# One layer in blocks of 768, 704 and 640 tokens with 47 ring tiles, column sums by transposition, shared tiles for the last norm and the plain gate in place

## The chip, the core and the metric

The kernel is one program on one core of a Trainium2 chip. The metric is the device time of one execution in microseconds (us). A core has five engines with instruction queues of their own: TensorE (PE, matmuls; the profile lists its weight loads as PEld), VectorE (DVE), ScalarE (ACT), GpSimd (POOL) and SyncE (SP). SP and POOL also issue nearly all DMA transfers here: SP the weights, POOL everything with a token dimension (spills to and reloads from DRAM, inputs, outputs).

## What is computed

One layer runs over 2048 prompt tokens and, with its own state, over 64 sample tokens. All data is float32, D_MODEL = 1024.

```python
h = rms_norm(x, g_pre)
vA, bA, cA, zA, q, f, iv, zB, gA, gB = split_cols(h @ w_in)        # ten pieces of 1024 columns
u = cA * vA;  conv = causal_conv3([conv_hist, u], conv_w)
yA = (silu(zA) * bA * conv) @ w_a_out
fg = lb + (1 - lb) * sigmoid(f);  logf = log(fg);  kk = 1 - fg;  qq = silu(q) * 128**-0.5
# 8 heads of 128 x 128, chunks of 64 tokens, state S carried from chunk to chunk:
#   att = tril(qe ke^T);  o = att v + (q exp b) S;  S = exp(b_last) S + (k exp(b_last - b))^T v
o = o * rsqrt(mean(o * o) + EPS) * g_onorm
yB = (o * silu(zB)) @ w_b_out
out = (sigmoid(gA) * yA + sigmoid(gB) * yB) @ w_o
x = x + rms_norm(out, g_post)
x = x + (p @ w_ple_proj) * sigmoid(rms_norm(x, g_ple) @ w_ple_gate)
```

The outputs are x for both sequences, the last two rows of u and the last S of each.

## The kernel before, in words

**Layout.** Everything is kept feature-major: a tile has 128 features (partitions) by the tokens of a block. The tokens stand in one row of 2112: prompt tokens up to CUT, then the 64 sample tokens, then the rest of the prompt. `plan()` (L46) cuts this row into NB = 3 blocks of BN = 704 tokens, each of two halves of HN = 352. A block's tokens fall into chunks of 64, and its `groups` are pairs of chunks (128 tokens) and, where a run has an odd number of chunks, one single. With CUT = 1344 each block has five pairs and one single. `parts` are up to four pairs, or one single: three parts a block (4 pairs, 1 pair, 1 single).

**Ring.** Nearly all working tiles come from one pool, `ring` (RING = 52 tiles of 708 columns, taken with `rt()`), and smaller half-wide ones from `hf()` (9). A new tile takes over the place of one that is no longer read; its first writer, a DMA among them, waits for that one's last reader. PSUM has five banks for gemms (`ps_gemm`) and three for the rest (`ps_attn`).

**Gemms.** Each float32 product is made of three fp32r matmuls: both operands are split into a rounded `hi` and a remainder `lo` (`split`, L188), and hi\*hi + hi\*lo + lo\*hi are summed. A group of two column blocks by one 1024-deep operand is computed in seven half-size products in place of eight (`sgroup`, L349, matmuls L363 to L365; `in_turn`, matmuls L496 to L498, takes whole stages product by product). `gemm` and its relatives use eight (`mm3`, L529 to L531), `plain_group` too (L433 to L435). Weights come as `raw` tiles by SP, ACT casts them to `hi` (L218), and their `lo` comes from DRAM where an earlier block has written it; block 0 makes the `lo` parts and the weight sums and writes them out. `prepare_sums` makes the sums of w_a_out and w_b_out (during block 0), w_o and w_ple_gate (beside `path_a` of blocks 1 and 2): POOL loads four tiles per group, DVE combines them (L337 to L343), POOL writes them out.

**Stages of a block.** (1) `gates`: sigmoid(gA) and sigmoid(gB), spilled; a number of these groups, LEAD = 7, runs at the end of the block before, the others fill in between the heads. (2) `path_b`: for each of 8 heads two sgroups (`head_prep`), and `head_attn` in four steps for every part: transposes of kb and vt and the scores (L925 to L952), state updates (L958 to L979), outputs and their norm (L994 to L1003), transposition back (L1008). The steps are `hooks`: one is called after each of the products of later sgroups, so attention matmuls stand between gemm matmuls, in PE's order. (3) `path_a`: 8 times two sgroups, with the convolution. (4) W_A, W_B, W_O: in block 0 plain gemms (`merge`, `final_out`), in block 1 W_A and W_B `in_turn` and W_O plain, in block 2 all `in_turn`. During W_O the next block's operands are made (`operands`: x loads at L643, scaling at L693, splits), the last two column blocks of W_O going k by k, so that the operand tiles of `mg` come free one k after the other. (5) `final_norm`: two norms with `rms` (`col_rstd`, `spread`); each step is a hook of the next block's gates. (6) the gate gemm W_G: for block 0 plain in `final_gate` after LEAD gates; for block 1 plain, at the end of block 2; for block 2 `in_turn` (`gate_in_turn`). Ahead of block 0 stands a prologue with the PLE gemms of blocks 0 and 1 (L1058 to L1060).

**Norms.** `col_rstd` (L614) sums the 128 partitions of a tile by matmuls with a column of ones as the moving operand, one per 128 tokens (L620), so that the sums come out as columns of PSUM, from which DVE and POOL make 1/sqrt. `spread` (L599) transposes the columns back over all partitions. `final_norm` of the last block runs once for each half, each with its own acc2, rs, rs2 and its own x tiles.

**Order.** `behind_all`, `placed` and `paced` put instructions behind named others in an engine's order. Each engine runs its queue in that order.

## Time and profile before

| | |
|---|---|
| median of three timed runs | 2609.88 us (2609.3 to 2610.56) |
| profiled execution | 2611.61 us, its span 2609.9 us |
| mean granted TensorE clock | 1.000 |
| DMA over the span | 745.99 MB, mean 286 GB/s |

How to read the rows shown below. A window row has: the stretch in us, its length, then for PE, PEld, DVE, ACT and POOL the busy time and, in brackets, how many instructions ran, then the granted clock, the mean busy share of the 16 DMA engines (which can pass 1 where packets overlap) and GB/s. A group row has: line, engine, operation, output<-inputs, shapes, xcount, then busy us and mean ns of one, then the idle time before them and what ended it. A row of waits reads: engine, what waited, what it waited for, us in total, how often, the longest. A timeline row has start, duration, instruction and, in brackets, the idle time before it and what ended it. Matmuls overlap in the pipeline, so their durations are longer than their spacing. A float32 matmul that isn't fp32r shows as two records, a transposition and an fp32r matmul as one.

### The profile page before, as it was taken

How to read it: one execution, taken by the hardware profiler on the slowest of the kernel's cores; microseconds unless marked ns; L12 is line 12 of the kernel's file. 1: busy time of each engine (PE TensorE's matmuls, PEld its weight loads, DVE VectorE, ACT ScalarE, POOL GpSimd, SP SyncE). 2: the span in 40 equal slices, each digit the busy share in tenths (PEclk: the TensorE clock that was granted, in tenths of full speed). 3: DMA queues.
4: the chain of work that ended last, by engine and by line, in shares of the span. 5: the costliest groups of instructions: out<-in, count | busy, mean ns of one | idle time of the engine just before them, and what ended most of it. 6: DMA issues, size and time to landing. Idle time of an engine off the chain costs nothing.

```text
span 2609.9 us, 47443 instructions
## 1 busy us (share of the span) xinstructions
PE 2588.6 (99%) x16562; PEld 2572.5 (99%) x16562; DVE 1667.1 (64%) x3232; ACT 1538.9 (59%) x2940; POOL 392.6 (15%) x722
## 2 busy tenths in 40 slices
PE   8999999999999999999999999999999999999999
PEld 8999999999999999999999999999999999999998
DVE  8778888888766555455545568553455544568756
ACT  6666665554434644677745556466667744555746
POOL 2000000200441212101112211021000101210220
PEclk9999999999999999999999999999999999999999
DMA  7687787898988997777789989599776789999977
GB/s 285 234 275 259 251 285 257 306 318 286 342 292 285 351 320 259 248 231 224 226 288 359 381 311 312 193 359 358 229 230 220 224 256 335 377 321 309 339 256 240
DMA packets 362672, 745.99 MB, mean 286 GB/s; under 512 B 44640, under 2 KB 49280, under 8 KB 362432
## 3 DMA queue, kind: packets, MB, share of 16 engines
q1 hardware_dynamic: 319680, 579.55, 65.4%
q0 software_dynamic: 42464, 163.37, 17.0%
q8 instruction: 130, 2.13, 0.3%
q14 instruction: 110, 0.90, 0.1%
q10 hardware_dynamic: 288, 0.05, 0.0%
HBM read 531.74 MB, written 211.04 MB: 285 GB/s over the span
## 4 chain that ended last, share of the span: by engine, by line
PE 89%; DMA 3%; DVE 2%; issue 2%; ACT 1%; POOL 1%; DVEq 0%; POOLq 0%; ACTq 0%; SPq 0%
PE pg L363 19%; PE pg L365 19%; PE pg L364 19%; PE pg L496 4%; PE pg L497 4%; PE pg L498 4%; PE pg L530 4%; PE pg L531 4%; PE pg L529 4%; PE pa L994 1%; PE pa L958 1%; PE pa L996 1%; PE pa L944 1%; DMA r<-w_blk 1%; DMA raw<-S 1%
## 5 line engine op out<-in xcount | busy, mean ns | idle before, releaser
L363 PE MATMUL pg<-r,hi 128*128 128x352 f32 x3304 | 1092.9, 331 | 4.6 <-DVE r L409 3.1
L364 PE MATMUL pg<-r,hi 128*128 128x352 f32 x3304 | 1067.6, 323 | 0.0
L365 PE MATMUL pg<-r,lo 128*128 128x352 f32 x2356 | 762.1, 323 | 1.2 <-DMA lo<-low 1.2
L218 ACT CAST hi<-raw 128x512 fp32r<-128x512 f32 x720 | 445.0, 620 | 499.8 <-PE pg L364 165.6
L363 PEld LDWEIGHTS pg<-r,hi 128*128 128x128 f32 x3304 | 622.2, 188 | 9.1 <-DVE r L409 3.2
L364 PEld LDWEIGHTS pg<-r,hi 128*128 128x128 f32 x3304 | 622.2, 188 | 0.0
L365 PEld LDWEIGHTS pg<-r,lo 128*128 128x128 f32 x2356 | 442.3, 188 | 1.8 <-DMA lo<-low 1.7
L365 PE MATMUL pg<-r,s 128*128 128x352 f32 x948 | 306.2, 323 | 0.1
L530 PE MATMUL pg<-r,hi 128*128 128x352 f32 x768 | 248.4, 324 | 0.0
L529 PE MATMUL pg<-r,hi 128*128 128x352 f32 x768 | 248.1, 323 | 0.0
L188 ACT CAST hi<-raw 128x512 fp32r<-128x512 f32 x218 | 134.6, 621 | 153.1 <-PE pg L364 53.5
L188 DVE TENSOR_TENSOR r<-r,r 128x352 fp32r<-128x352 f32 (+3 forms) x298 | 182.8, 637 | 62.7 <-ACT r L188 61.7
L497 PE MATMUL pg<-r,hi 128*128 128x352 f32 x672 | 217.3, 325 | 0.0
L496 PE MATMUL pg<-r,hi 128*128 128x352 f32 x672 | 213.6, 325 | 0.1
L531 PE MATMUL pg<-r,lo 128*128 128x352 f32 x656 | 211.9, 323 | 0.1
L188 ACT CAST r<-r 128x352 fp32r<-128x352 f32 (+3 forms) x298 | 162.2, 580 | 56.9 <-DVE r L1114 15.4
L188 DVE TENSOR_TENSOR lo<-raw,hi 128x512 fp32r<-128x512 f32 x218 | 149.4, 687 | 63.5 <-ACT hi L188 55.2
L365 PEld LDWEIGHTS pg<-r,s 128*128 128x128 f32 x948 | 178.4, 188 | 0.4 <-DMA s<-low 0.4
L188 ACT CAST hi<-s 128x512 fp32r<-128x512 f32 x160 | 98.5, 621 | 123.0 <-PE pg L364 105.8
L377 ACT COPY hf<-pg 128x352 f32<-128x352 f32 x354 | 157.1, 446 | 11.5 <-PE pg L365 10.9
L530 PEld LDWEIGHTS pg<-r,hi 128*128 128x128 f32 x768 | 144.3, 188 | 0.3 <-DVE r L188 0.2
L529 PEld LDWEIGHTS pg<-r,hi 128*128 128x128 f32 x768 | 144.2, 188 | 0.0
(367 smaller groups left out, 4157.0 us busy)
## 6 DMA issues: line engine op xcount, KB each, us to landing
raw<-w_blk SPq DMA_DIRECT2D x570, 256.0 KB, 4.2
lo<-low SPq DMA_DIRECT2D x411, 256.0 KB, 4.4
raw<-S SPq DMA_DIRECT2D x408, 256.0 KB, 4.4
low<-lo SPq DMA_DIRECT2D x314, 256.0 KB, 3.7
s<-low SPq DMA_DIRECT2D x309, 256.0 KB, 4.2
S<-s SPq DMA_DIRECT2D x152, 256.0 KB, 3.2
r<-w_blk POOLq DMA_DIRECT2D x64, 256.0 KB, 7.3
S<-r POOLq DMA_DIRECT2D x64, 256.0 KB, 5.8
```

The costliest lines, as they stand in the source:

```text
L188: return A.copy(hi, src).ins, V.tensor_tensor(lo, src, hi.bitcast(F32), ALU.subtract).ins
L218: A.copy(hi, raw)
L363: add(hi[:, k, :], xhi, start=start and k == 0, stop=False)
L364: add(hi[:, k, :], xlo, start=False, stop=False)
L365: last[0] = add(lo[:, k, :], xhi, start=False, stop=k == KH - 1).ins
L377: copied = A.copy(got[n], ps[bank])
L496: add(hi[:, k, :], xhi, start=start and k == 0, stop=False)
L497: add(hi[:, k, :], xlo, start=False, stop=False)
L498: last[0] = add(lo[:, k, :], xhi, start=False, stop=k == KH - 1).ins
L529: T.matmul(ps, hi[:, k % 4, :], xhi[:, c], start=k == ks[0], stop=False)
L530: T.matmul(ps, hi[:, k % 4, :], xlo[:, c], start=False, stop=False)
L531: last[0] = T.matmul(ps, lo[:, k % 4, :], xhi[:, c], start=False, stop=k == ks[-1]).ins
```

## The change

Blocks get sizes of their own, 768, 704 and 640 tokens, with CUT = 1408; all widths follow from the block at hand (`wide`, set by `width_of` and `of_block`), tiles are as wide as the widest block (772 columns), and there are 47 of them. The groups become 6 pairs; 5 pairs and the sample's single; 5 pairs, in parts of 4 + 2, 4 + 1 + single, 4 + 1. Four places follow suit: `head_prep` handles any even number of pairs in its swapped layout, `head_attn` copies v that way for parts of two, the scores of a single pair go to the first slot of `att`, and the first head of block 0 has two empty hooks instead of one after its third step.

Besides, `col_rstd` transposes tiles and lets DVE reduce them; the two halves of the last block's norm share acc2, rs, rs2 and full-width x tiles, which the first half loads; `final_gate` multiplies and adds in the tile of `p`, half by half with an `hf` tile for the sigmoid, and asks for x when the gemm begins instead of one gemm ahead.

```diff
-CUT = 1344
-BN = 704
-HN = BN // 2
-NB = TOK // BN
-RING = 52
+SIZES = (768, 704, 640)
+CUT = SIZES[0] + SIZES[1] - DEC
+BMAX = max(SIZES)
+HMAX = BMAX // 2
+RING = 47
...
-    def rt(n=BN, dt=F32):
-        t = ring.tile([P, BN + 4], dt, tag="r", name=nm("r"))
-        return t if n is None else t[:, :n]
+    def rt(n=None, dt=F32):
+        return ring.tile([P, BMAX + 4], dt, tag="r", name=nm("r"))[:, : n or wide[0]]
...
         with placed():
             for i, o in tiles_of(n):
-                T.matmul(pc[:, i : i + 1], acc[:, o : o + P], ones, start=True, stop=True)
-        rstd_of(pc[:, : cols.shape[1]], cols, 1.0 / D)
+                T.transpose(pc[:, i * P : i * P + P], acc[:, o : o + P], ident)
+        nt = cols.shape[1]
+        V.tensor_reduce(cols, cols3(pc, nt), axis=mybir.AxisListType.X, op=ALU.add)
+        rstd_of(cols, cols, 1.0 / D)
...
-            V.tensor_tensor(kb[:, 4 * P :], sf[:, 4 * P :], lg[:, 4 * P :], ALU.mult)
...
+            if n > nsw * P:
+                V.tensor_tensor(kb[:, nsw * P :], sf[:, nsw * P :], lg[:, nsw * P :], ALU.mult)
...
+            if npair > nsw:
+                rest = kb[:, nsw * P : np1].rearrange("p (g c t) -> p g c t", c=2, t=CH)[:, :, 0, :]
+                V.tensor_tensor(rest, ka3[:, nsw:npair, :], f2[:, nsw:npair].unsqueeze(2).to_broadcast([P, 1, CH]), ALU.mult)
+                if nch == 2 * npair:
+                    V.memset(ka[:, nch // 2 * CH : nch // 2 * CH + CH], 0.0)
...
                 if step == 2:
-                    hooks.append(None)
+                    hooks.extend([None] * (2 if first and hd == 0 else 1))
...
-        acc2, rs, rs2 = rt(), rt(), rt()
-        xks = []
-
-        def fetch():
-            j = len(xks)
-            if j < KB:
-                xks.append(rt())
-                G.dma_start(xks[j][:, c], x_fm[j * P : (j + 1) * P, segs[0]["t0"] : segs[0]["t0"] + n])
-
-        for _ in range(3 if bl["last"] else 4):
-            fetch()
+        (acc2, rs, rs2), xks = common["tiles"], common["xks"]
+        ahead = 3 if bl["last"] else 4
+
+        def fetch(upto):
+            while len(xks) < min(upto, KB):
+                xks.append(load_x(bl, len(xks)))
+
+        fetch(ahead)
...
-        def fetch(j):
-            return [reload(kept[kind, j]) for kind in "xp"] if j < KB else None
-
-        nxt = fetch(0)
+        nxt = reload(kept["p", 0])
         for j in range(KB):
+            pj, xj = nxt, reload(kept["x", j])
             pss = gemm(W_G + j, h2, segs)
-            (xj, pj), nxt = nxt, fetch(j + 1)
-            t = rt()
+            nxt = reload(kept["p", j + 1]) if j + 1 < KB else None
             for s, ps in zip(segs, pss):
-                A.activation(t[:, cols_of(s)], ps, AF.Sigmoid)
-            V.tensor_tensor(t, pj, t, ALU.mult)
-            V.tensor_tensor(t, t, xj, ALU.add)
-            queue.dma_start(y_fm[j * P : (j + 1) * P, bl["t0"] : bl["t0"] + BN], t)
+                gate = hf()
+                A.activation(gate, ps, AF.Sigmoid)
+                V.tensor_tensor(pj[:, cols_of(s)], pj[:, cols_of(s)], gate, ALU.mult)
+            V.tensor_tensor(pj, pj, xj, ALU.add)
+            queue.dma_start(y_fm[j * P : (j + 1) * P, bl["t0"] : bl["t0"] + bl["n"]], pj)
...
                 if (idx, n) == (W_O, 4):
-                    norms = [final_norm(bl, [s], xo, acc, h2, None, True) for s in segs]
+                    common = {}
+                    norms = [of_block(bl, final_norm(bl, [s], xo, acc, h2, None, True, common)) for s in segs]
```

## The prediction

> **What bounds the kernel now.** I read the page's busy times and its chain of waits first, then PE's own waits, then a window in which PE never stops.

> ```profile
> span 2609.9 us, 47443 instructions
> PE 2588.6 (99%) x16562; PEld 2572.5 (99%) x16562; DVE 1667.1 (64%) x3232; ACT 1538.9 (59%) x2940; POOL 392.6 (15%) x722
> PE 89%; DMA 3%; DVE 2%; issue 2%; ACT 1%; POOL 1%; DVEq 0%; POOLq 0%; ACTq 0%; SPq 0%
> ...
> PE pa L1058 <- ACT r L188: 6.6, 1, 6.6
> PE pg L363 <- DVE r L409: 3.1, 9, 0.6
> PE pa L1008 <- DVE r L1003: 1.7, 1, 1.7
> PE pg L363 <- ACT hi L218: 1.5, 2, 0.7
> ...
> 550.00:600.00 50.00, 50.00 (x312) 50.00 (x311) 43.92 (x73) 24.42 (x45) 1.27 (x4) 1.00 0.86 291
> ```

> TensorE is the bound: 89% of the chain, 99% busy, and its four longest waits make only 12.9 us. So the time is a sum over matmul records, each at its spacing from start to start (the durations in the groups overlap). The window gives 50.00 / 312 = 160.3 ns for a gemm matmul of 352 columns. The change is worth the change of that sum, plus whatever PE then waits for. The profiled execution took 2611.6 us (span 2609.9); the timed runs have their median at 2609.9, 1.7 below it, and I carry the difference over to the median. A measurement here can tell about 0.2%, 5.2 us, from no change.

> **Columns: +3.1 us.** The blocks stay three, so the number of gemm matmuls stays and only their widths move. Counted in the loops, in triples like L363 to L365: block 0 has 1064 by seven products, 64 in plain_group, 512 in plain gemms (W_A, W_B, W_O, W_G) and 32 for PLE, 1672; block 1 has 1120 + 224 + 256 + 32 = 1632; block 2, by seven products throughout, 1120 + 448 + 32 = 1600. The group agrees with its share: 1064 + 1120 + 1120 = 3304.

> ```profile
> L364 PE MATMUL pg<-r,hi 128*128 128x352 f32 x3304 | 1067.6, 323 | 0.0
> ```

> Widths go from 352 everywhere to 384, 352, 320: 3 x 32 x (1672 - 1600) = 6912 columns more, because the widest block is the one that skips the seven-product scheme most. At 160.3 / 352 = 0.455 ns a column, +3.1. Were a part of the spacing fixed, at most the 0.11 us that 128-column records take (next rows), the slope would be (160.3 - 110) / (352 - 128) = 0.22 ns and the price +1.6. I take 3.1, since this shape's own row gives it.

> **Attention groups: -9.7 us.** Today each block has five pairs of chunks and one single; after, the blocks have 6 pairs, 5 pairs and a single, 5 pairs. Per head two singles go and one pair comes. Either costs 11 PE records: three transposes of one record (L925, L927, L1008) and four matmuls of two (L944, L958, L994, L996); the number of L943 matmuls stays.

> ```profile
> 304.13 0.32 PE L365 MATMUL pg<-r,lo 128*128 128x352 f32 x1
> 304.30 0.61 PE L994 MATMUL pa<-r,att 128*128 128x128 f32 x4
> 304.74 0.39 PE L996 MATMUL pa<-r,r 128*128 128x128 f32 x2
> 304.96 0.39 PE L994 MATMUL pa<-r,att 128*128 128x128 f32 x2
> 305.19 0.39 PE L996 MATMUL pa<-r,r 128*128 128x128 f32 x2
> ...
> L994 PE MATMUL pa<-lone,att 128*128 128x128 f32 x48 | 9.2, 273 | 0.0
> ```

> Four records take 304.74 - 304.30 = 0.44 us, two 0.22: 0.11 a record. 8 heads x 11 x 0.11 = 9.7. DVE and ACT lose the singles' work too, which hides behind PE anyway. With two parts rather than three, p_o and the transpose of its norm (L1008) stand three hooks apart instead of four. In between run Square, reduce, pow and multiply:

> ```profile
> L1000 ACT ACTIVATE r<-pa 128x512 f32<-128x512 f32 x24 | 14.4, 600 | 14.7 <-PE pa L996 14.7
> L1001 DVE TENSOR_REDUCE ms<-r 128x4 f32<-128x512 f32 x24 | 16.5, 686 | 30.5 <-ACT r L1000 30.5
> L593 POOL TENSOR_TENSOR ms<-ms,mhalf 128x4 f32<-128x4 f32 (+2 forms) x72 | 53.1, 738 | 295.3 <-DVE ms L591 293.6
> L1003 DVE TENSOR_TENSOR r<-pa,ms 128x512 f32<-128x512 f32 x24 | 16.6, 692 | 27.2 <-POOL ms L593 27.2
> ```

> That is 2.7 us; three hooks are 36 matmuls, 5.2 us even at 320 columns. Covered; without the cover it would be a stall at each of 8 heads. Block 0's first head gets one empty hook more: it is the head where PE waits 1.7 us for L1003 today. I book -1.7 (0 if the chain is late again).

> **Column sums: -4.6, and +0.5 in the prologue.** A matmul against `ones` runs as two records, a transpose as one: 84 become 42, 42 x 0.11 = 4.6.

> ```profile
> L620 PE MATMUL pa<-ones,r 128*128 128x1 f32 x84 | 10.1, 244 | 0.1
> L1001 DVE TENSOR_REDUCE ms<-lone 64x1 f32<-64x128 f32 x24 | 6.8, 283 | 0.8
> ```

> The 14 new reduces over 3x128 lie between 283 and 686 ns, about 0.55 us each, and wait in DVE's order. Twelve stand behind hooks with gemm work around them. Two stand in the prologue, where the first matmul waits 6.6 us anyway: exposed they cost 1.1, hidden 0; with the 9% wider first loads and splits I take +0.5 (0 to 2).

> [...]

> **Head starts of block 0: -1.** PE waits 3.1 us in nine places for DVE's sink (L409). With 9% more time per product and no single to serve, DVE gains room; 0 to -3.1, I take -1.

> **Gate in place, shared norm tiles: 0.** The plain gate splits one DVE multiply into halves, beside 24 matmuls per half gemm. Its x is asked for only when its own gemm starts, and a gemm (48 matmuls at 175 ns) takes 8.4 us:

> ```profile
> r<-x POOLq DMA_DIRECT2D x16, 352.0 KB, 5.4
> ```

> 5.4 us lie behind that. If a tile comes late, DVE is late, and next ACT's `hf` tiles, nine of them; PE is reached last. The last norm's second half loads no x of its own, 8 issues less on POOL's queue.

> **DMA in block 2: +5.6.** Block 2's matmuls get 9% faster, but each still needs the same weight bytes. Two stretches have the DMA engines full already:

> ```profile
> 1700.00:1800.00 100.00, 99.89 (x629) 99.10 (x628) 47.48 (x76) 59.71 (x110) 21.82 (x38) 1.00 1.02 381
> 2200.00:2300.00 100.00, 98.98 (x613) 98.46 (x612) 54.49 (x94) 50.97 (x99) 21.44 (x44) 1.00 1.02 378
> ...
> 1740.00:1750.00 10.00, 10.00 (x64) 10.00 (x63) 4.42 (x9) 6.03 (x13) 1.62 (x3) 1.00 1.04 405
> 1780.00:1790.00 10.00, 10.00 (x64) 10.00 (x63) 2.71 (x5) 4.84 (x10) 1.22 (x3) 1.00 1.04 406
> ...
> DVE r L337 <- DMA r<-w_blk: 51.3, 10, 8.7
> ```

> The first is block 1's norm (x loads, two spills a tile) beside block 2's first gates. Its 38.1 MB, of which only the gates' spills shrink (0.5 MB), would have to pass in 90.9 us, 414 GB/s. At some 400, just below the fullest rows, they take 94.0: +3.1 of lost gain. The second is prepare_sums beside path_a: 37.8 MB at 400 take 94.5, +3.6; part may slip, as W_G needs the sums much later, but DVE stands up to 8.7 us before L337 and its sinks queue behind it, so I take +2.5. Ends: 0 each (all of it slips), 9.1 each (no gain at all).

> **Ring of 47: +2.** Near the end of W_O, counted in the code, live tiles are 16 of mg, 7 for each finished pair of the next block's operands, 11 for the pair in work, xo and the sums. The last pair's x loads wait for PE to release mg:

> ```profile
> 830.54 1.07 POOL L643 DMA_DIRECT2D r<-x_fm  x2 [28.38 <-PE pg L531]
> 1677.62 1.07 POOL L643 DMA_DIRECT2D r<-x_fm  x2 [28.36 <-PE pg L531]
> 840.75 0.94 DVE L693 SCALAR_TENSOR_TENSOR r<-r,vec,r 128x704 f32<-128x704 f32 x1
> 844.95 0.51 ACT L188 CAST r<-r 128x352 fp32r<-128x352 f32 x1
> ...
> 851.26 0.43 PE L363 MATMUL pg<-r,hi 128*128 128x352 f32 x1 [0.74 <-ACT hi L218]
> ```

> Each k of the by-k gemm releases two tiles in 12 matmuls, 1.9 us (2.1 in block 0). Five tiles fewer put the loads 2.5 steps, about 5 us, later, and POOL's norm loads behind them. x is scaled at 841.7 and ACT casts it only at 844.95, behind other work: 3.2 us of cover. So some 1.8 us a block end, twice, less 1.4 for block 0's longer steps: +2. Ends: 0, and 10 with the cover gone.

> **Sum:** 3.1 - 9.7 - 1.7 - 4.6 + 0.5 - 1 + 5.6 + 2 = -5.8. 2611.6 - 5.8 = 2605.8 for the profiled execution, 2604.1 for the median: **2604**.

> **Rivals.** *The DMA engines hold block 2 back* (slower). If they pass no more than the 381 and 378 GB/s of both stretches, PE keeps its old pace there: 2 x 9.1 instead of 5.6, +12.6, **2617**. It decides once the ceiling lies below some 385. For it: a share of 1.02 over whole stretches; against: 405 for ten microseconds. [...] *The ring exposes the block ends*: +10 for +2, **2612**; for it the waits of 28 us, against it the 3.2 us of cover. *Nothing comes in the way*: 5.6 and 2 fall to 0, **2596**; for it that PE stood 0.1 us in all between 1700 and 1800. *Block 2's matmuls don't get shorter*, so that the change doesn't do what it says: 4800 x 14.6 ns more, **2674**; the 0.11 of narrower records speaks against a floor at 160. *Losses that only offset the gain*, several of these in part: **2609**.

> **Chances.** Forecast 0.38, nothing in the way 0.14, ring 0.18, DMA 0.17, offset 0.11, no shorter matmuls 0.02. The forecast's own spread, 2599 to 2608, leaves three quarters of it beyond 5.2 us: faster 0.14 + 0.28 = 0.42; slower 0.17 + 0.02 + half the ring's 0.09 = 0.28; same the rest, 0.30. Range 2595 to 2618: it takes in all but the far end of each unknown cost.

> **What would show it.** Spacing of 175, 160 and 146 ns in plain stretches of the three blocks; 88 records fewer in attention (L994's `lone` form x16 for x48), 42 transposes for L620; no wait before L1008. DMA: gaps of PE in block 2's first gates and in path_a, ended by DMA or L409, over 5.6 us in all mean the rival. Ring: L643's last loads later than one k into W_O's last gemm, and a PE gap in each next block's first product over 1 us. The prediction is wrong if those gaps exceed the 14 us that the shorter record list saves, or if the spacing at 320 stays near 160.

## The result and the profile after

The change makes the kernel slower by about 0.2%: 2615.88 us median of 17 runs (2612.61 to 2618.3) against 2610.55 of 17 runs of the kernel before (2607.92 to 2613.15), a ratio of 1.002 with the interval 1.0012 to 1.0027. The profiled execution took 2618.3 us, its span is 2616.6.

From the page of the changed kernel, its span, the busy times and the engines' shares of the chain that ended last; below them the longest of TensorE's own waits (engine, tile and line, what it waited for, us in total, times, the longest):

```profile
span 2616.6 us, 47076 instructions
PE 2584.3 (99%) x16432; PEld 2564.4 (98%) x16432; DVE 1648.8 (63%) x3165; ACT 1525.9 (58%) x2908; POOL 376.6 (14%) x698
PE 82%; DMA 5%; ACT 4%; DVE 3%; issue 2%; POOL 1%; ACTq 0%; POOLq 0%; SPq 0%; DVEq 0%
```

```profile
PE pa L1084 <- ACT r L207: 6.9, 1, 6.9
PE pg L384 <- DMA lo<-low: 4.1, 3, 2.2
PE pg L382 <- DVE r L429: 3.8, 4, 1.8
PE pa L953 <- DVE r L429: 2.0, 7, 0.3
PE pa L624 <- POOL cols L613: 1.8, 6, 0.5
PE pg L549 <- ACT r L207: 1.6, 2, 1.2
```

TensorE runs 130 matmul records fewer and is busy 4 us less, yet the span is 6.7 us longer. Its share of the chain fell from 89% to 82%; DMA, ScalarE and VectorE took the difference. The waits ahead of L384, L953, L624 and L549 are new or longer; the one ahead of block 0's first norm transposes (L1008 before, L1034 now) is gone.

Windows of the changed kernel without a gap, one in each block, then the two stretches of block 2 that the prediction called full (us; length; busy time and instructions of PE, PEld, DVE, ACT, POOL; granted clock; DMA share; GB/s):

```profile
500.00:550.00 50.00, 50.00 (x287) 50.00 (x287) 41.20 (x74) 26.67 (x57) 5.21 (x10) 1.00 0.86 298
1380.00:1430.00 50.00, 50.00 (x317) 49.93 (x316) 21.93 (x48) 25.45 (x54) 9.78 (x20) 1.00 0.86 294
1830.00:1880.00 50.00, 50.00 (x343) 50.00 (x342) 18.38 (x32) 30.20 (x56) 7.57 (x14) 1.00 1.04 391
...
1770.00:1860.00 90.00, 86.85 (x583) 85.59 (x582) 46.66 (x77) 54.68 (x104) 21.26 (x37) 0.98 1.01 384
2230.00:2330.00 100.00, 95.55 (x636) 94.38 (x635) 56.37 (x101) 51.21 (x102) 21.44 (x45) 0.98 1.04 389
```

The matmuls did get their forecast pace, 50 / 287 = 174 ns, 158 and 146 ns (the second has a few records of attention in it; the median spacing there is 161). In the two stretches where the DMA engines are full (share 1.01 and 1.04, 384 and 389 GB/s), TensorE now stands for 3.1 and 4.5 us.

**A wait that the sum did not have.** In block 2, each head's transposes of vt (L953) wait for VectorE. The timeline of the changed kernel at one head (start, us, engine and line, idle before in brackets):

```profile
2022.91 0.82 DVE L908 TENSOR_TENSOR r<-r,qc 128x640 f32<-128x640 f32 x1
...
2023.27 0.60 PE L951 MATMUL pa<-ident,r 128*128 128x128 f32 x4
...
2024.06 0.48 DVE L429 TENSOR_TENSOR r<-hf,hf 128x320 f32<-128x320 f32 x1
2024.19 0.84 PE L953 MATMUL pa<-ident,r 128*128 128x128 f32 x4 [0.33 <-DVE r L429]
...
2026.13 0.40 PE L382 MATMUL pg<-r,hi 128*128 128x320 f32 x1
```

VectorE is still at the end of `scaled` (L908) when TensorE is done with the head's last product, so the two adds that make vt (L429) come late: the second ends 1.27 us after L951's start. In the kernel before, the same add (L409 there) ended 0.86 us ahead of the transposes of kb:

```profile
2008.00 0.52 DVE L409 TENSOR_TENSOR r<-hf,hf 128x352 f32<-128x352 f32 x1
...
2009.38 0.60 PE L925 MATMUL pa<-ident,r 128*128 128x128 f32 x4
2009.81 0.60 PE L927 MATMUL pa<-ident,r 128*128 128x128 f32 x4
```

From L951 to the next product (L382) the burst takes 2026.13 - 2023.27 = 2.86 us; an undisturbed one 2.14 (below, one_slot). Seven of block 2's eight heads pay this, 4.9 us in all; the sum of the 24 bursts of this kind, eight in each block, rose from 51.1 to 56.0 us.

**A stall that costs more than itself.** Windows of 2 us around the longest gap in block 2's path_a (1.83 us idle ahead of 2294.62, ended by L429):

```profile
2290.00:2292.00 2.00, 2.00 (x14) 1.80 (x13) 0.76 (x2) 0.18 (x1) 0.00 (x0) 1.00 1.05 384
2292.00:2294.00 2.00, 0.79 (x6) 0.52 (x4) 1.93 (x4) 0.62 (x1) 1.44 (x3) 1.00 1.06 388
2294.00:2296.00 2.00, 1.38 (x8) 1.41 (x9) 1.85 (x5) 0.00 (x0) 0.72 (x2) 0.85 1.04 391
2296.00:2298.00 2.00, 2.00 (x9) 2.00 (x9) 1.08 (x2) 1.98 (x4) 0.18 (x1) 0.50 1.05 416
2298.00:2300.00 2.00, 2.00 (x13) 2.00 (x12) 1.23 (x3) 1.52 (x5) 0.00 (x0) 0.79 1.04 410
```

After the gap the granted clock is 0.50 for 3.4 us: nothing is waited for, PE is busy throughout, and 9 matmuls fit into 2 us where 14 did (267 ns each). The changed kernel's trace has three such spells after its start (1701, 1803 and 2295 us), each right behind a gap of over 2 us (2.47 and 2.15 from start to start) or behind several close together; the trace of before has none between its start and its last matmul. Each costs about 1.5 us: some 12 matmuls stand at half clock throughout and take 120 ns more each, 1.44, and the two at its ends add about 0.1.

### The profile page after: what moved, and what is told of

Same layout as the page of the kernel before. It is cut to its first block, busy times and chain, and to the rows that moved or that the text cites. A ratio compares the mean times of both kernels' runs of the same rounds, so it can differ in the third digit from the quotient of the medians.

```text
span 2616.6 us, 47076 instructions
## 1 busy us (share of the span) xinstructions
PE 2584.3 (99%) x16432; PEld 2564.4 (98%) x16432; DVE 1648.8 (63%) x3165; ACT 1525.9 (58%) x2908; POOL 376.6 (14%) x698
## 4 chain that ended last, share of the span: by engine, by line
PE 82%; DMA 5%; ACT 4%; DVE 3%; issue 2%; POOL 1%; ACTq 0%; POOLq 0%; SPq 0%; DVEq 0%
PE pg L382 16%; PE pg L383 16%; PE pg L384 16%; PE pg L551 5%; PE pg L550 5%; PE pg L549 5%; PE pg L516 4%; PE pg L517 4%; PE pg L518 3%; DMA raw<-S 2%; DMA r<-w_blk 1%; PE pa L984 1%; PE pa L1020 1%; PE pa L970 1%; ACT hi L237 1%
## 5 line engine op out<-in xcount | busy, mean ns | idle before, releaser
L382 PE MATMUL pg<-r,hi 128*128 128x320 f32 (+2 forms) x3304 | 1087.5, 329 | 5.5 <-DVE r L429 3.8
L383 PE MATMUL pg<-r,hi 128*128 128x320 f32 (+2 forms) x3304 | 1069.3, 324 | 0.0
L384 PE MATMUL pg<-r,lo 128*128 128x384 f32 (+2 forms) x2356 | 766.9, 326 | 4.1 <-DMA lo<-low 4.1
L382 PEld LDWEIGHTS pg<-r,hi 128*128 128x128 f32 x3304 | 622.6, 188 | 7.9 <-issue 4.7
L383 PEld LDWEIGHTS pg<-r,hi 128*128 128x128 f32 x3304 | 622.7, 188 | 0.2 <-DVE r L207 0.2
L384 PEld LDWEIGHTS pg<-r,lo 128*128 128x128 f32 x2356 | 443.2, 188 | 5.1 <-DMA lo<-low 5.1
L384 PE MATMUL pg<-r,s 128*128 128x352 f32 (+1 forms) x948 | 299.3, 316 | 1.0 <-DMA s<-low 1.0
L549 PE MATMUL pg<-r,hi 128*128 128x384 f32 (+1 forms) x768 | 256.1, 334 | 1.6 <-ACT r L207 1.6
L550 PE MATMUL pg<-r,hi 128*128 128x384 f32 (+1 forms) x768 | 256.1, 334 | 0.1
L207 ACT CAST hi<-raw 128x512 fp32r<-128x512 f32 x218 | 134.7, 620 | 178.2 <-PE pg L550 57.9
L207 DVE TENSOR_TENSOR r<-r,r 128x320 fp32r<-128x320 f32 (+7 forms) x298 | 182.0, 633 | 64.9 <-ACT r L207 63.9
L551 PE MATMUL pg<-r,lo 128*128 128x384 f32 (+1 forms) x656 | 219.9, 335 | 0.0
L517 PE MATMUL pg<-r,hi 128*128 128x320 f32 (+1 forms) x672 | 211.1, 316 | 0.2 <-DVE r L207 0.2
L516 PE MATMUL pg<-r,hi 128*128 128x320 f32 (+1 forms) x672 | 206.0, 316 | 0.9 <-ACT r L207 0.8
L207 DVE TENSOR_TENSOR lo<-raw,hi 128x512 fp32r<-128x512 f32 x218 | 149.3, 686 | 63.1 <-ACT hi L207 60.4
L207 ACT CAST r<-r 128x320 fp32r<-128x320 f32 (+7 forms) x298 | 161.0, 576 | 46.0 <-DVE r L715 12.7
L207 ACT CAST hi<-s 128x512 fp32r<-128x512 f32 x160 | 98.0, 618 | 145.7 <-PE pg L383 130.8
L384 PEld LDWEIGHTS pg<-r,s 128*128 128x128 f32 x948 | 178.5, 188 | 1.8 <-DMA s<-low 1.8
L396 ACT COPY hf<-pg 128x352 f32<-128x352 f32 (+2 forms) x354 | 156.7, 444 | 3.8 <-PE pg L384 3.6
L207 DVE TENSOR_TENSOR lo<-s,hi 128x512 fp32r<-128x512 f32 x160 | 110.1, 689 | 68.9 <-ACT hi L207 67.3
L549 PEld LDWEIGHTS pg<-r,hi 128*128 128x128 f32 x768 | 144.8, 189 | 2.2 <-ACT r L207 2.2
```

Of the source, the lines that this page charges most:

```text
L207: return A.copy(hi, src).ins, V.tensor_tensor(lo, src, hi.bitcast(F32), ALU.subtract).ins
L382: add(hi[:, k, :], xhi, start=start and k == 0, stop=False)
L383: add(hi[:, k, :], xlo, start=False, stop=False)
L384: last[0] = add(lo[:, k, :], xhi, start=False, stop=k == KH - 1).ins
L396: copied = A.copy(got[n], ps[bank])
L516: add(hi[:, k, :], xhi, start=start and k == 0, stop=False)
```

## The experiments

Two theories of the loss were put to the test, with rivals. *Covers*: work of nearly fixed length on ScalarE, VectorE and the DMA engines lay hidden behind TensorE's products; products that are 9% shorter, in a block of two attention parts, no longer hide it. Against it: the ring of 47, the column sums by transposition, or DMA alone. Ratios are to the kernel before.

| run | blocks, and what differs from the change | median us | ratio, interval |
|---|---|---|---|
| after_again | none | 2615.97 | 1.0019, 1.001 to 1.0028 |
| old_sizes_52 | 3 x 704, ring 52 | 2612.29 | 0.9998, 0.999 to 1.0007 |
| old_sizes_47 | 3 x 704 | 2611.8 | 1.0001, 0.9992 to 1.001 |
| ones | column sums by ones | 2620.74 | 1.0027, 1.0017 to 1.0037 |
| one_slot | one empty hook slot | 2610.75 | 0.9993, 0.9984 to 1.0002 |
| one_slot_sums | and earlier weight sums | 2609.08 | 0.9994, 0.9985 to 1.0003 |
| sums_first | and priority for L642, L611 | 2609.42 | 0.9991, 0.9982 to 0.9999 |
| no_x | one_slot without 8 loads | 2613.37 | 1.0011, 1.0002 to 1.002 |
| mid640 | 768, 640, 704 | 2629.81 | 1.0075, 1.0062 to 1.0088 |
| rev | 640, 704, 768 | 2626.72 | 1.0059, 1.0046 to 1.0071 |

### The old sizes, with both rings

```
-SIZES = (768, 704, 640)
+SIZES = (704, 704, 704)
-HMAX = BMAX // 2
+HMAX = BMAX // 2 + 32
-RING = 47
+RING = 52          (old_sizes_52; 47 kept in old_sizes_47)
```

> The changed kernel with three blocks of 704 tokens and 52 ring tiles again; what stays of the change is the column sums by transposition, the shared tiles of the last norm and the gate in place. Covers theory (the loss of the change comes with block 2's shorter products, which no longer cover the fixed chains of ScalarE, VectorE and the DMA): the gaps ahead of L953 in block 2's heads are gone, the time is that of the kernel before less the 1.3 us that the trace shows for the column sums, 2609 us, ratio 0.9995 within 0.0007. Column-sum theory (the longer chain of reduction, power and spread costs more than the matmuls with ones saved): 2613 us or more, ratio 1.001 or more. If the column sums gave the 4.6 us of the forecast: 2606 us, ratio 0.998.

> The same with 47 ring tiles, so that the ring alone differs from the former run. Covers theory: no tile is missed where the blocks end, but where more than 47 were live (block 0's last gate, the output product of block 1) some splits come late: at most 2.5 us over the former run, ratio of the two below 1.001, about 2611 us. Ring theory (the ring of 47 is the loss of the change): 4 us or more over the former run, 2613.5 us or more, with the gaps at the first products of block 1's output stage.

With the old sizes the loss is gone, with either ring. So it comes with the sizes, and neither the column sums, the shared tiles and the gate in place taken together nor the ring shows in the time. The ring does leave a trace, not at the block ends but in block 1's W_O: of TensorE's waits in old_sizes_47 this one has no counterpart in old_sizes_52,

```profile
PE pg L549 <- ACT r L207: 1.2, 1, 1.2
```

and it is followed by a spell at half clock (1632 us, 1.46 us lost). The medians don't show these 2.7 us; executions of one kernel differ by more (those of the kernel before by 5.2 us).

### The column sums by ones again

```
+    ones = const.tile([P, 1], F32, tag="ones", name="ones")
+    V.memset(ones, 1.0)
...
-                T.transpose(pc[:, i * P : i * P + P], acc[:, o : o + P], ident)
-        nt = cols.shape[1]
-        V.tensor_reduce(cols, cols3(pc, nt), axis=mybir.AxisListType.X, op=ALU.add)
-        rstd_of(cols, cols, 1.0 / D)
+                T.matmul(pc[:, i : i + 1], acc[:, o : o + P], ones, start=True, stop=True)
+        rstd_of(pc[:, : cols.shape[1]], cols, 1.0 / D)
```

> The changed kernel with the column sums by matmuls with a column of ones again, nothing else. Covers theory: the sum bursts cost 1.3 us more and the waits for the spread's transposes on GpSimd and VectorE go, net 2616 to 2618 us, ratio to the kernel before 1.002 to 1.003; the gaps ahead of L953 stay. Column-sum theory: 2613 us or less, ratio 1.001 or less.

Not faster, so the transposition isn't the loss. The ratio lies in the forecast of the covers theory, the median 2.7 us above it; the interval overlaps that of the change, and the trace has the seven waits ahead of L953 unchanged (0.47 to 0.62 us from start to start).

### One empty slot

```
-hooks.extend([None] * 3 if first and hd == 0 else [])
+hooks.extend([None] * 3 if first and hd == 0 else [None] * 1 if len(attn) == 2 and not first else [])
```

> The changed kernel with one empty hook slot ahead of the attention steps of every head of a block of two parts other than the first (block 2), so that its first transposes come a product's part (36 matmuls, about 5.2 us) later and the bursts lie that much further back; nothing else changes. Covers theory: the waits ahead of L953 go, the eight heads' bursts fall from 56.0 us towards the 51.2 us of before, 2611 us, ratio to the kernel before 1.000 within 0.0007. If DMA or ring hold the change back: no change, 2615 to 2616.5 us, ratio 1.002, with the waits moved to other lines of the same heads.

A slot is one product of 12 matmuls, 1.8 us in block 2; the 36 matmuls in the expectation are three slots. The same head in one_slot's timeline:

```profile
2023.68 0.60 PE L951 MATMUL pa<-ident,r 128*128 128x128 f32 x4
2024.12 0.60 PE L953 MATMUL pa<-ident,r 128*128 128x128 f32 x4
...
2025.82 0.40 PE L382 MATMUL pg<-r,hi 128*128 128x320 f32 x1
```

No wait: 2.14 us for the burst, 51.1 us for all 24. The median is 5 us below that of the change, the whole loss, though not the gain that was forecast: the cover theory holds for this wait. The profiled span fell by 3.4 only, for in that execution 2.5 us more went into waits ahead of the column sums (L640, 0.6 to 3.1 us).

### Where the short block lies

```
-SIZES = (768, 704, 640)
+SIZES = (768, 640, 704)          (mid640)
+SIZES = (640, 704, 768)          (rev)
```

> The changed kernel with blocks of 768, 640 and 704 tokens: the short products lie in block 1, and both later blocks have three attention parts, which fill all 14 slots of a head. By the matmul spacings (175, 147 and 161 ns on 5016, 4896 and 4800 matmuls) the columns cost 1.3 us less than in the changed kernel, one more part in eight heads some 4 us more. If two parts in a block without fills are the cause of the waits ahead of L953: no such waits in any block, 2610 us, ratio 0.9995 within 0.001. If short products alone are the cause: the waits of 0.3 to 0.5 us per head stand in block 1, some 4 us, 2614 us or more, ratio 1.001 or more.

> The changed kernel with its sizes in the reverse order, 640, 704 and 768 tokens: by the same spacings the columns cost 6 us less than in the changed kernel (2365.6 against 2371.7 us), and block 2, with two parts as before, has products 19% longer. Covers theory: the waits ahead of L953 and the DMA's gaps in block 2 go, 2600 to 2605 us, ratio 0.997 within 0.001. Against it: block 0, where VectorE is busiest (87% in the page's early slices), gets short products and becomes VectorE's; then the gaps with VectorE as releaser in block 0's heads rise by more than 6 us and the time is 2611 us or more, ratio 1.000 or more. If two parts alone make the waits: they stand in block 2 with these sizes too, 8 of 0.3 us or more.

In mid640, block 1 has two groups of 64 tokens, which share the tiles for single groups, so one of them is computed with the other's keys and values, and L1034 waits 0.6 us per head for them; for the rest it is comparable. The covers theory's forecasts of the time fell in both runs (2610 us, and 2600 to 2605); what rev's expectation held against it came true, VectorE's waits in block 0. About the wait ahead of L953 the runs are clear, though: it stands neither in mid640 (short products with three parts; vt is ready 0.35 us ahead of L951) nor in rev's block 2 (two parts with long products; 0.24 to 0.75 us ahead). It takes two parts and short products, and a third thing: rev's block 0 has two parts and 320 columns as well and doesn't wait for vt. There a gate group stands between a head's products and its attention (three empty slots in the first head), and vt is ready 0.9 us or more ahead. In block 2 only the first head has such a group, and it is the one of the eight that doesn't wait.

The times show a larger effect of the same kind. Of rev's TensorE waits:

```profile
PE pg L384 <- DVE lo L207: 10.7, 11, 2.4
PE pg L382 <- DVE r L429: 8.5, 8, 1.3
...
PE pg L549 <- ACT hi L207: 3.6, 2, 2.4
```

```profile
450.00:550.00 100.00, 90.78 (x578) 87.82 (x578) 80.24 (x149) 51.43 (x112) 9.46 (x21) 0.97 0.86 294
```

VectorE, which also splits block 0's weights (L207), needs 0.69 us per weight tile with either block size; with products of 320 columns TensorE overtakes it. The window lies in block 0; PE is busy for 91% of it. In rev's block 2, with its long products, TensorE has no gap of over 0.2 us beyond the spacing in the first gates and in path_a, where the changed kernel loses 8.1 us. mid640 puts the short products against block 1's DMA traffic instead: gaps of 2.46, 1.83 and 3.82 us there, ended by DMA or by L429, and four spells in the run, at least 7 us lost. Of the three places for the short block, block 2 costs least.

### The DMA engines in block 2

```
-                if j >= 3:
+                if j >= 3 if nxt else j in (0, 2, 4, 5, 6):
                     next(sums_, None)
```

> As one_slot, and in block 2's path_a the five steps that prepare the last gate's weight sums are taken at products 0, 2, 4, 5 and 6 instead of 3 to 7, so that their 12.6 MB (48 transfers of 256 KB) move over the whole of path_a and not over its last 100 us, where the DMA's busy share is 1.04. Covers theory with the DMA as its second part: the gaps of some 5 us in that stretch fall to about 1.5 us, 2607 us, ratio to the kernel before 0.998. If it is VectorE's work and not the transfers that is late there: no change against one_slot, 2610.5 us, ratio 0.9993.

In the trace the gaps of path_a fell from 5.2 us beyond the spacing (five gaps in one_slot) to 2.6 (four), and the run has no spell. Windows of both stretches, one_slot's path_a first, then that of one_slot_sums:

```profile
2230.00:2330.00 100.00, 95.65 (x646) 94.42 (x646) 60.56 (x109) 53.80 (x109) 21.38 (x44) 1.00 1.02 382
```

```profile
2220.00:2320.00 100.00, 98.36 (x669) 97.63 (x667) 53.80 (x96) 52.71 (x105) 18.72 (x40) 1.00 1.01 369
```

At 369 GB/s in place of 382, TensorE's idle time goes from 4.4 to 1.6 us. The waits there are called VectorE's (L429), but VectorE stood 6.35 us ahead of 2291.20, in its order before the late adds, for a weight tile:

```profile
2291.20 0.69 DVE L356 TENSOR_TENSOR r<-r,r 128x512 f32<-128x512 f32 x1 [6.35 <-DMA r<-w_blk]
```

(from the changed kernel's timeline). So it is a DMA wait passed on through VectorE's queue. The medians, 0.9994 and 0.9993, do not confirm a gain of 3 us, nor exclude it.

```
-            while len(xks) < min(upto, KB):
+            while (bl["last"] or kept is None or not raw) and len(xks) < min(upto, KB):
...
-            V.tensor_tensor(xj, xj, xks[j][:, c], ALU.add)
+            V.tensor_tensor(xj, xj, xks[j][:, c] if xks else xj, ALU.add)
```

> As one_slot, and block 1's last norm doesn't load x again (8 transfers of 352 KB fewer, about half of them in block 2's first gates): it adds the normalized row to itself in place of x, so block 1's rows lack the residual; VectorE's instructions stay. If the DMA engines at their ceiling (busy share 1.01, 381 GB/s) are what holds TensorE in block 2's first gates: the gaps between 1790 and 1885 us, 5.5 us in one_slot, fall below 2.5 us, ratio 0.998. If it is the first gates' order of loads alone (weights that are asked for late): the gaps stay above 4 us, ratio 0.9993.

The waits for DMA in the first gates fell from 2.7 us beyond the spacing (three gaps in one_slot, 1800 to 1816 us) to 1.1 (two), and L640's wait behind them stayed at 1.4 to 1.5. The profiled span is 4.7 us below one_slot's, but the median lies 2.6 above it, against the forecast. I have no explanation for that; this run doesn't settle the first gates.

### Room for the column sums

In one_slot's timeline of VectorE, in the last norm:

```profile
2488.90 0.55 DVE L642 TENSOR_REDUCE cols<-pa 128x3 f32<-128x384 f32 x1
2490.82 0.49 DVE L661 TENSOR_TENSOR r<-r,r 128x320 f32<-128x320 f32 x1 [1.37 <-ACT r L660]
2491.24 0.48 DVE L1227 TENSOR_TENSOR r<-r,r 128x320 f32<-128x320 f32 x1
2491.64 0.48 DVE L661 TENSOR_TENSOR r<-r,r 128x320 f32<-128x320 f32 x1
2492.04 0.16 DVE L611 TENSOR_SCALAR cols<-cols 128x3 f32<-128x3 f32 x1
```

The reduction takes its 0.55 us, as forecast; but it splits a step in two, and the planner put other work between the halves, one instruction of it waiting for ScalarE.

```
-        V.tensor_reduce(cols, cols3(pc, nt), axis=mybir.AxisListType.X, op=ALU.add)
-        rstd_of(cols, cols, 1.0 / D)
+        with tc.high_priority():
+            V.tensor_reduce(cols, cols3(pc, nt), axis=mybir.AxisListType.X, op=ALU.add)
+            rstd_of(cols, cols, 1.0 / D)
```

> As one_slot_sums, and in the column sums by transposition the reduction (L642) and the scaling (L611) are given priority, so that VectorE takes L611 behind at most one other instruction; in one_slot three instructions of the last norm stand between them, one of which waits 1.37 us for ScalarE, L611 starts 3.1 us after its reduction, and TensorE waits 2.06 us for GpSimd's power ahead of the spread (L624). If the longer chain is what took the gain of the column sums: the gap at about 2486 us and the one at about 2460 us fall below 0.8 us together, 2607 us, ratio to the kernel before 0.9985. If it is GpSimd's power or the hook's place: the gaps stay at 1.8 us or more, ratio 0.9993.

The gap at 2486 us is gone (1.31 us from start to start in one_slot_sums), that at 2462 us is as before (0.51), so together they are below 0.8 us, as the first forecast said. But TensorE's waits for the power ahead of the spread don't end with it; one_slot_sums first, then sums_first:

```profile
PE pa L624 <- POOL cols L613: 2.5, 6, 1.0
PE pa L624 <- POOL cols L613: 1.5, 5, 0.5
```

The priority removed one of them and left the rest as they were. This version is faster than the kernel before by 0.09%, which is little over what its interval can tell (0.9982 to 0.9999), and it can't be told apart from one_slot_sums.

> The changed kernel unaltered, beside the variants of this call: 2614 to 2617 us, ratio to the kernel before 1.002; its eight heads in block 2 wait ahead of L953 again (bursts 56 us against 51.2), and what one_slot and one_slot_sums gained shows as a ratio below 1 of those runs to this one.

It repeats: 1.0019, with the waits ahead of L953 (block 2's large bursts take 21.9 us again, 17.0 in the kernel before). The ratios of one_slot, one_slot_sums and sums_first lie below it with intervals that don't touch its own.

### What a stall costs

```
...
+                if n == 0 and stall:
+                    with tc.high_priority():
+                        V.tensor_copy(stand, got[n])
+                        for _ in range(stall - 1):
+                            V.tensor_tensor(stand, stand, stand, ALU.max)
+                    pa = ps_attn()
+                    with placed():
+                        held_up[0] = tc.issue_after(T.transpose(pa[:, :P], stand[:, :P], ident).ins)
...
```

(in the sgroup for FF and QQ of each head of blocks 1 and 2, in the kernel before; the next product is issued behind the transpose).

> The kernel before with 51 ring tiles and one made stall of TensorE in each head of blocks 1 and 2 (16 in all): after the first product of the head's first group, VectorE passes the product's copy 2, 3, 4 or 5 times over a small tile (heads 0 to 3 and again 4 to 7), and TensorE transposes that tile before it goes on. By the durations of such copies (0.5 to 0.6 us each) the gaps are about 1.7, 2.1, 2.6 and 3.0 us. Clock theory (after a gap of some 2 us the granted clock falls to a half for about 3.2 us, which costs 1.44 us more, by chance of where the gap falls): no spell after the 1.7 us gaps, spells after some of the 2.1 and 2.6 us gaps and after most of 3.0 us, 6 to 10 spells of 16; without it the spells of the changed kernel come from something else, and there are none here. [...]

> The same with 6, 4, 3 and 2 passes (gaps of about 3.5, 2.6, 2.1 and 1.7 us) in heads 0 to 3 and again 4 to 7, so that other moments are hit. Clock theory: a spell after each of the four gaps of 3.5 us, after some of 2.6 and 2.1 us, after none of 1.7 us.

These two missed their doses: the made gaps were 0.83 us from start to start with 5 passes, 1.39 with 6 (less in the first head of a block), none with fewer, because the chain on VectorE began before TensorE came to it. Another wait appeared in most heads, 1.41 us for ScalarE's copy. No spell followed any of the 27 gaps of about 1.4 us; three followed gaps of 2.27, 2.72 and 1.64 us that the kernel had of itself. Times: 2641.85 us (ratio 1.0124, 1.0107 to 1.0141) and 2647.9 in one run.

> As stalls_a, with 7, 8, 9 and 10 passes in heads 0 to 3 and again 4 to 7. In the two runs before, a pass took 524 ns and 5 and 6 passes made gaps of 0.83 and 1.39 us at the made stall, so these make about 1.9, 2.4, 3.0 and 3.5 us. Clock theory: no spell at half the clock after gaps of 1.4 us, a spell of 3.2 us after some of the 1.9 and 2.4 us gaps and after most of 3.0 and 3.5 us, 8 to 14 spells of 16. [...]

> The same with 10, 7, 8 and 9 passes, so that each dose falls at other moments. Clock theory: as many spells, 8 to 14, each dose's share like that of the run before within two. [...]

Two of the stalls in stalls_c, of 7 passes (its row and the windows behind it) and of 8 passes (the windows from 1216 us on):

```profile
1179.03 0.30 PE L395 MATMUL pa<-ident,stand 128*128 128x128 f32 x1 [1.63 <-DVE stand L392]
```

```profile
1178.00:1180.00 2.00, 0.97 (x9) 1.00 (x10) 0.84 (x2) 0.20 (x1) 0.00 (x0) 1.00 0.97 343
1180.00:1182.00 2.00, 2.00 (x18) 2.00 (x17) 0.48 (x1) 1.39 (x4) 0.00 (x0) 1.00 0.27 101
...
1216.00:1218.00 2.00, 0.05 (x1) 0.08 (x2) 1.70 (x4) 0.30 (x1) 0.00 (x0) 1.00 0.85 285
1218.00:1220.00 2.00, 2.00 (x11) 2.00 (x12) 0.00 (x0) 0.69 (x2) 0.00 (x0) 0.56 0.29 111
1220.00:1222.00 2.00, 2.00 (x13) 2.00 (x12) 0.00 (x0) 1.00 (x3) 0.00 (x0) 0.59 0.00 0
```

Counted over both runs, by the gap from matmul start to matmul start: 1.92 to 2.01 us, no spell after 8 stalls; 2.51 to 2.53 us, after 6 of 7; 3.03 to 3.08 us, after 8 of 9; 3.63 us, after 6 of 6. (Two of the 32 stalls fell apart into shorter gaps; most of the others, short and long ones, have the gap of 1.4 us ending about 2 us ahead of them.) The spells last 3.4 us at half clock, twice 6.8. The two executions took 2696.4 and 2690.59 us.

The traces also show where the spells lie. Within each trace all of them start whole multiples of 3.413 us apart (in the changed kernel at 1701.49, 1803.89 and 2295.41 us: 30 and 144 times 3.413, and each lasts 3.413 us). So a trace can be divided into stretches of that length that begin where its spells begin. Windows of the changed kernel, the three stretches ahead of its spells and the one with the most idle time among the others:

```profile
1698.08:1701.49 3.41, 1.69 (x7) 0.94 (x6) 3.23 (x8) 1.27 (x4) 0.54 (x1) 1.00 0.94 327
1800.48:1803.89 3.41, 1.33 (x9) 1.33 (x10) 1.57 (x3) 0.95 (x2) 1.08 (x2) 1.00 1.03 405
2292.00:2295.41 3.41, 1.57 (x11) 1.34 (x10) 3.29 (x6) 0.62 (x1) 2.17 (x4) 1.00 1.06 390
2261.28:2264.69 3.41, 2.11 (x15) 1.85 (x14) 0.44 (x1) 1.16 (x2) 0.00 (x0) 1.00 1.04 405
```

TensorE's records leave 1.72, 2.08 and 1.84 us of the first three idle, 1.30 of the last. In the trace of before, divided the same way from the spell behind its last matmul, no stretch between start and end has over 1.19. Counted over all 16 traces, start, end and the spells themselves left aside: where 1.9 us or more of a stretch is idle, a spell follows in 32 of 32; from 1.3 to 1.9 us in 9 of 42; below that in none of some 12,100. Both long stalls without a spell, of 2.52 and 3.03 us, lie across the border of two stretches (both in stalls_d: at 1096 us, with some 1.8 us idle in one and 0.4 in the next, and at 1838 us, with 1.2 and 1.5), and so do gaps of 2.56, 2.71 and 2.73 us without one in old_sizes_47, ones and old_sizes_52. A shorter gap in the changed kernel, of 2.15 us and within one stretch (the third row), was followed by a spell.

## Why the prediction was wrong

The time lies in the range, the direction is wrong: -5.8 us forecast, +5.3 measured. By the terms of the sum, with the two traces set side by side, each gap or burst counted beyond the block's spacing:

| term | forecast | traces |
|---|---|---|
| columns | +3.1 | +1.2 |
| attention groups | -9.7 | -9.6 |
| first head's wait | -1.7 | -1.9 |
| head starts of block 0 | -1 | -2.4 |
| column sums | -4.6 | -1.5 |
| DMA in block 2 | +5.6 | +6.7 |
| ring | +2 | +2.8, in W_O of block 1 |
| waits ahead of L953 | not seen | +4.9 |
| last output stage | not seen | +2.6 |
| half clock after gaps | not seen | +4.1 |

That adds up to +6.9 where the spans differ by 6.7. The columns go by mean spacings over stretches of 60 and more matmuls without a break, 161.07 ns before, 175.06, 161.18 and 146.58 after; 0.1 ns in one of them is 0.5 us here, so the close agreement is partly chance. The half clock counts the matmuls that stand in it throughout. The prologue, +0.5 in the forecast, is not in the table: it grew by 0.6 to 0.9 us, and the stretch behind the last matmul's start shrank by 0.6. The spells differ from one execution to the next.

**Right:** the bound, the spacings (to 1 ns), the record count (130 fewer; 42 transposes in L640, 16 records in L1020's `lone` form), the end of the wait at L1008, and DMA in block 2 within 1.1 us. The lines of the chain behind p_o were read with a slip that changes nothing: the power (L593) was taken at the mean of three shapes, 738 ns, where the 128x4 one takes 1112, so the chain is 3.1 us, still under 5.2.

**The step that failed** is the sentence on attention with two parts: "three hooks are 36 matmuls, 5.2 us even at 320 columns. Covered; without the cover it would be a stall at each of 8 heads". The kind of loss was right, a stall at the heads (seven of eight pay it, 4.9 us), but it looked only at the chain inside a part (L1000 to L1003). The chain that lost its cover lies ahead of the part's first step: `scaled` and the adds of vt on VectorE, which ended 0.86 us ahead of the burst before and end 1.27 us into it after. The last product ahead of the burst shrank by only 0.16 us (12 matmuls, 1.92 to 1.76); how the rest divides between the head's other products and the steps of the third part is not shown. One_slot shows that a product's time is what is missing: with 12 matmuls more ahead of the burst, the wait is gone.

**The columns' gain was never the point; the rows' loss was.** Every stretch of block 2 was priced for DMA alone. The same 9% had to be held against VectorE's chains there too, and rev and mid640 show the other two blocks have still less room.

**Stalls were priced at their own length.** The prediction had no term for the clock, though all its windows carry the column. Of the made stalls, those of 2.5 us cost about 1.5 more in 6 of 7 cases. Over the 17 timed executions of the change, the granted clock was 0.998 in three (2617.2 us on average), 0.999 in eleven (2615.4) and 1.000 in three (2614.4): the spells are part of the loss, but some 4 us of it remain without them.

**Column sums** were a mis-sized term, -1.5 for -4.6: the records went as counted, but longer waits ahead of the spread (L624), for GpSimd's power, gave 2.9 us of it back at five places. The extra instruction's place in VectorE's order is shown for one of them, the one at 2486 us that priority removed (0.5 us in the changed kernel); at the other four, 2.4 us, it is open whether the reduction's own 0.55 us or the hook's place is the cause. **The ring's** price was about right and its place wrong: both block ends kept their gaps (1065 and 1061 ns before, 1060 and 1239 after), and late splits in block 1's W_O appeared. That the ring is their cause rests on one pair of traces.

Of the rivals, "DMA" (2617) and "ring" (2612) came nearest in time, and that is luck: the DMA engines cost 6.7 us where the rival had 18.2, the ring 2.8 where it had 10. By the prediction's sign the DMA rival held, though (gaps in the first gates and path_a of over 5.6 us; they make 8.1), and the stretches ran at 384 and 389 GB/s, between its 381 and 378 and the sum's 400. In kind "offset", several losses in part, fits best, but it had them cancel the gain only. All of TensorE's gaps together, beyond the spacing, rose by 14.9 us, from 12.5 in 22 gaps to 27.4 in 42; the gaps that the prediction named as its sign of being wrong, those of DMA and ring, stay below its 14.

## What to carry to other kernels

When a tile gets shorter, list for its stage every chain whose length does not shrink with it (here table loads of 1.28 us, GpSimd's power of 1.1, weight splits of 0.69, weight tiles of 256 KB, the same in both kernels), and hold each against the shortened cover, starting with the first step behind a reshuffled schedule and not only with the steps that changed. A slot left empty in the new schedule may be worth more at its front than at its end. An instruction split in two gives the planner a place to put other work: look at what lands between.
